# The first 45 microseconds of a two-layer trunk: load queues, zero products, and where layer 0's norm is summed

## The chip, the cores and the metric

The kernel runs on one core of a Trainium2 chip. The core has five engines that run side by side, each with its own ordered stream of instructions: TensorE (PE in the profile) for matrix products and transposes, VectorE (DVE), ScalarE (ACT) and GpSimd (POOL) for elementwise work, and SyncE (SP), which here only issues transfers. ACT and POOL can issue transfers too. An instruction waits for semaphores of the engines and transfers that it depends on, and whatever stands behind it on its engine waits with it.

The metric is the device time of one execution in microseconds, as the median of the runs. Before the change it is 995.59 us, over three runs of 995.08, 995.59 and 996.93 us.

## The reference, cut to what matters

The computation is a two-layer decoder trunk on 512 tokens of 1024 channels, in float32. Each layer has a mixer and a gated feed-forward network, each behind an RMS norm, and a last norm follows. The change touches layer 0's mixer only:

```python
xn = rms_norm(h, norm_mix[0])                 # h = x, the input
proj = jnp.einsum('bsd,de->bse', xn, w_in_even[0])        # 1024 -> 2048
a_b, a_c, a_v, z_b = proj[..., 0:512], proj[..., 512:1024], proj[..., 1024:1536], proj[..., 1536:]
y_a = a_b * causal_dwconv3(a_c * a_v, conv_a[0])
y_b = multiscale_pool(z_b, w_pool[0], pool_scale[0])      # windows 2, 4, 8, 16, one per group of 128 channels
h = h + jnp.einsum('bse,ed->bsd', jnp.concatenate([y_a, y_b], -1), w_out_even[0])
```

`multiscale_pool` takes for each group of 128 channels the mean over the last 2, 4, 8 or 16 tokens, less the token itself, and multiplies the result by a 128 x 128 matrix.

## The kernel before, in words

Activations are kept with channels on the 128 partitions and the 512 tokens along the row, so the 1024 channels are eight tiles, `k` = 0 to 7. Every float32 factor is split into a rounded high part and a low part (the residue), and a product of two tiles is three TensorE products: high by high, low by high and high by low (`mm3`, lines 146 to 149). ACT makes the high parts, DVE the low ones. A product accumulates in one of seven PSUM banks (`mm_bank`); an eighth, `aux_bank`, is for small things.

Work is written down in one order, and a scheduler orders each engine's instructions by priority and readiness within what the data allow. Instructions passed through `inorder` (or `order`) keep the order in which they were written on their engine. `behind` puts one instruction behind another on the same engine.

The kernel begins with eight products on zeros (the tile `idle`, lines 53 to 57), which nobody reads. Then layer 0's mixer (`mixer0`) starts:

- `load` fetches `x` in pieces (one tile, one tile, then pairs) and the matching rows of the weights of the z columns (1536 to 2047 of `w_in_even`). x goes over SP's queue. The first two weight pieces, z0 and z1, go over ACT's queue, the pairs over SP's. The norm's gain (`params_fetch`, 8 rows of 128) is fetched over ACT's queue behind z0.
- `turn(k)` transposes tile k of x on TensorE (four transposes of 128 x 128), turns the gain for k = 0, lets ACT write the high parts of the weights (`whi_z`) and of the scaled x (`hgh`) and DVE the low ones (`wlo_z`, `hgl`), copies x to `h`, and has ACT square a tile. POOL adds the squares up in `ssq`.
- `z_first` runs the products of k = 0 and 1 over the four column groups of z, with `turn(k + 1)` after the first four of each k. The general loop (`group`) does the rest, with `turn(k + 1)` ahead of each k. The last two k are done one column group after the other, so the four groups end one by one; each time `z_done(g)` is called.
- The normalization is not applied ahead of the products: the reciprocal root of the mean square is taken while they run. `rstd_cols` sums `ssq` over partitions by eight small products (the tile `ssc`, line 220) and takes the root on columns (ACT's square root, then DVE). `rstd_spread` turns the columns into a tile of all tokens by four transposes (`ssr`, line 210). Both use the `aux` bank. In `z_done`, `rstd_cols` is called at g = 1, `rstd_spread` and the pooling of groups 0 and 1 at g = 2, and the pooling of groups 2 and 3 behind their copies. `z_copy` takes a finished bank to SBUF on ACT; there are two such buffers. `z_pool` (DVE) scales it, builds the window sums by doubling, and splits the result into `pooled`.
- Then come the column groups `ac`, `av` and `ab` (512 columns each, with the same `group` loop over all eight k and the last four k done column by column). `c_done` evacuates `ac` on DVE (line 474), which needs the spread norm. Their weights come in four pieces of two k each into four `raw` buffers, which the splits free again.

Of the kernel before, what the change touches and what calls it, by code (L numbers as in the profile page):

```python
# [8 lines left out]
F32 = mybir.dt.float32  # L9
# [6 lines left out]
P = 128  # L16
D = 1024
S = 512
NK = D // P
# [3 lines left out]
EPS = 1e-6  # L23
WINDOWS = (2, 4, 8, 16)
PAD = 16
WARM = 8
LINE = 64
SHARE = 672

# [2 lines left out]
def tile_trunk(ctx: ExitStack, tc: tile.TileContext, x, norm_mix, norm_ffn, final_norm,  # L32
# [3 lines left out]
    nc = tc.nc  # L36
# [9 lines left out]
    def mm_bank(name):  # L46
        return ps_mm.tile([P, 512], F32, tag="mm", name=name)

    def aux_bank(name):
        return ps_aux.tile([P, 512], F32, tag="aux", name=name)  # L50


    idle = tp.tile([P, 512], BF16, tag="rstd", name="idle")
    nc.vector.memset(idle, 0.0)
    clock = aux_bank("clock")
    for i in range(WARM):
        nc.tensor.matmul(clock, idle[:, :P], idle, start=i == 0, stop=i == WARM - 1)

    ident = cp.tile([P, P], F32, name="ident")
    make_identity(nc, ident)  # L60
# [9 lines left out]
    def params1():  # L70
# [1 line left out]
            ("mix", rows_of(norm_mix[1]), NK), ("bsp", b_spatial[0], NK),  # L72
            ("ffn", rows_of(norm_ffn[1]), NK), ("cf", conv_rows(conv_ffn[1]), 3 * NF),
            ("bf", rows_of(b_conv_ffn[1]), NF)])

    inorder = tc.keep_in_program_order

    def behind(ins, first):

# [13 lines left out]
    def params_fetch(layer, rows_, queue):  # L93
        rows = sum(n for _, _, n in rows_)
        pk = cp.tile([P, P], F32, tag="pk", bufs=1, name=f"pk{layer}")
        at, views = 0, {}
        for key, ap, n in rows_:
            queue.dma_start(pk[at : at + n, :], ap)
            views[key] = at
            at += n  # L100

        def turned(order=lambda ins: ins):
            ps = aux_bank(f"prm_ps{layer}")
            order(nc.tensor.transpose(ps[:, :rows], pk[:rows, :], ident[:rows, :rows]))
            sb = cp.tile([P, P], F32, tag="prm0" if layer == "0" else "prm1", name=f"prm{layer}")
            nc.vector.tensor_copy(sb[:, :rows], ps[:, :rows])

            def col(key, i):
                return sb[:, views[key] + i : views[key] + i + 1]

            return col

        return turned

    def rows_of(ap):
        return ap.rearrange("(r p) -> r p", p=P)
# [2 lines left out]
        return ap.rearrange("w (r p) -> (w r) p", p=P)  # L119


    def fetch(src, a, b, name, queue=nc.sync):
        raw = wp.tile([P, a, b], F32, tag="raw", bufs=4, name=f"raw_{name}")
        queue.dma_start(raw, src)
        return raw, a, b, name

    def weights(src, a, b, name):
# [52 lines left out]
    def hg_k(k):  # L180
        return hg[k][0], hg[k][1]
# [124 lines left out]

    prm0 = prm1 = None

    def in_fetch(name, w, c0, k, n, queue=nc.sync):
        return fetch(w[k * P : (k + n) * P, c0 : c0 + 512].rearrange("(k p) c -> p k c", p=P),  # L310
                     n, 512, f"{name}_{k}", queue)

    def in_parts(chunks, k, raw, after=(None, None)):
        hi, lo = parts(*raw, after=after)
# [3 lines left out]
    def in_group(name, w, c0, lhs_is_weight, on_done, tail, chunks=None, before=None,  # L318
                 after=(None, None), begun=None):
        if chunks is None:  # L320
            chunks = {}
            for k in range(0, NK, 2):
                in_parts(chunks, k, in_fetch(name, w, c0, k, 2), after)

        def wt(k, j):
            cs = slice(j * P, (j + 1) * P)
            return chunks[k][0][:, cs], chunks[k][1][:, cs]

        def wt_wide(k, j):
            return chunks[k]  # L330

        def tokens(k, j):
            cs = slice(j * P, (j + 1) * P)
            return hg[k][0][:, cs], hg[k][1][:, cs]

        if lhs_is_weight:
            group(name, range(4), list(range(NK)), wt, lambda k, j: hg_k(k), tail, on_done, before,
                  begun=begun)
        else:
            group(name, range(4), list(range(NK)), tokens, wt_wide, tail, on_done, before)  # L340

    def mixer0():
        nonlocal prm0
        w = w_in_even[0]
        with tc.tile_pool(name="m0", bufs=1) as mp:
            prm_mix = {}
            norm = Norm("m0", lambda k: prm_mix["col"]("mix", k))
            zchunks = {}
            xt = {}
# [1 line left out]
            def load(k, n):  # L351
                t = mp.tile([P, NT, n * P], F32, tag="four", bufs=5, name=f"xt{k}")
                nc.sync.dma_start(
                    t, x[:, k * P : (k + n) * P].rearrange("(t p) d -> p t d", p=P))
                for i in range(n):
                    xt[k + i] = t[:, :, i * P : (i + 1) * P]
                raws[k] = in_fetch("z", w, 1536, k, n, nc.scalar if n == 1 else nc.sync)
                if k == 0:
                    prm_mix["turned"] = params_fetch(
                        "mix", [("mix", rows_of(norm_mix[0]), NK)], nc.scalar)  # L360

            raws = {}
            fed = [None, None]
# [7 lines left out]
            def turn(k):  # L371
                ps = mm_bank(f"xt_ps{k}")
                order = inorder if k < 2 else lambda ins: ins
                for t in range(NT):
                    order(nc.tensor.transpose(ps[:, t * P : (t + 1) * P], xt[k][:, t, :], ident))
                if k == 0:
                    prm_mix["col"] = prm_mix["turned"](inorder)
                if k in raws:
                    raw, a, b, name = raws.pop(k)
                    hi = wp.tile([P, a, b], F32R, tag="whi", bufs=6, name=f"whi_{name}")  # L380
                    lo = wp.tile([P, a, b], F32R, tag="wlo", bufs=6, name=f"wlo_{name}")
                    for i in range(a):
                        zchunks[k + i] = hi[:, i, :], lo[:, i, :], raw[:, i, :]
                whi, wlo, wraw = zchunks[k]
                inorder(nc.scalar.activation(whi, wraw, AF.Copy))
                g = prm_mix["col"]("mix", k)
                inorder(nc.scalar.activation(hg[k][0], ps, AF.Copy, scale=g))
                inorder(nc.vector.tensor_tensor(wlo, wraw, whi.bitcast(F32), ALU.subtract))
                fed[0] = inorder(nc.vector.scalar_tensor_tensor(
                    hg[k][1], ps, g, hg[k][0].bitcast(F32), op0=ALU.mult, op1=ALU.subtract))  # L390
                inorder(nc.vector.tensor_copy(h[k], ps))
                if k > 0:
                    norm.square(k - 1, put_square)
                if k == 0:
                    load(6, 2)
                elif k == NK - 1:
                    norm.square(k, put_square)
# [19 lines left out]
            W = S + PAD  # L417
            mix = {}
# [3 lines left out]
            zs = {}  # L422

            def z_copy(g, ps):
                zs[g] = mp.tile([P, S + LINE], F32, tag="z", bufs=2, name=f"z{g}")[:, :W]
                nc.gpsimd.memset(zs[g][:, :PAD], 0.0)
                nc.scalar.copy(zs[g][:, PAD:], ps)

            def z_done(g, ps):
                if g == 1:  # L430
                    norm.rstd_cols()
                elif g == 2:
                    rstd[0] = norm.rstd_spread()
                    z_pool(0)
                    z_pool(1)
                z_copy(g, ps)
                if g > 1:
                    z_pool(g)

            def z_pool(g):  # L440
                win, z = WINDOWS[g], zs[g]
                nc.vector.tensor_tensor(z[:, PAD:], z[:, PAD:], rstd[0], ALU.mult)
                s, step = z, 1
                while step < win:
                    s2 = mp.tile([P, S + LINE], F32, tag="zs", bufs=3, name=f"zs{g}_{step}")[:, :W]
                    lo_c = 2 * step - 1
                    nc.vector.tensor_tensor(s2[:, lo_c:], s[:, lo_c:], s[:, lo_c - step : W - step],
                                            ALU.add)
                    s, step = s2, 2 * step
                pl = mp.tile([P, S], F32, tag="pl", bufs=2, name=f"pl{g}")  # L450
                nc.vector.scalar_tensor_tensor(pl, s[:, PAD:], 1.0 / win, z[:, PAD:],
                                               op0=ALU.mult, op1=ALU.subtract)
                e = win - 1
                nc.vector.tensor_tensor(pl[:, :e], s[:, PAD : PAD + e], inv_pos[:, :e], ALU.mult)
                nc.vector.tensor_tensor(pl[:, :e], pl[:, :e], z[:, PAD : PAD + e], ALU.subtract)
                pooled[g] = split(mp, pl, f"pl{g}", tag="mix", bufs=8)
# [11 lines left out]
            ac = {}  # L468
# [6 lines left out]
                nc.gpsimd.tensor_tensor(t, t, rstd[0], ALU.mult)  # L475
                ac[j] = t

            in_group("ac", w, 512, True, c_done, 4, after=fed)

            cv = {}  # L480

# [12 lines left out]
            for g in range(4):  # L494
                ps = mm_bank(f"pm{g}")
# [644 lines left out]
    def down(name, ks, pieces, lhs, rhs, on_done):  # L1140

        for n, piece in enumerate(pieces):
# [4 lines left out]
            on_done(piece, ps)  # L1147

    n = mixer0()
    n = ffn0(n)  # L1150
    n = mixer1(n)
# [31 lines left out]
```

## Time and profile before

| what | value |
|---|---|
| median of three runs | 995.59 us |
| the profiled execution's own time | 996.99 us |
| span of the profiled execution, first to last instruction | 995.3 us |
| TensorE busy | 984.4 us (99%) |
| DVE, ACT, POOL busy | 728.5, 535.8, 104.1 us |
| first product on zeros starts | 1.26 us |
| first transpose of x starts | 6.08 us |
| first z product starts | 8.34 us |
| first z product of k = 2 starts | 17.79 us in the chain |
| norm sums (`ssc`) start | 34.94 us |
| first `ac` product | 37.95 us in the chain |

Times in the profile count from the first instruction of the program. A row of the timeline has the start, the duration, the engine, the line, the operation and its tiles; products are pipelined, so each one's duration overlaps the next one's start. The chain follows what ended last back to what released it, and gives each piece only the time that it added. A row of the waits has who waited for whom, the microseconds in total, how often, and the longest. Each row is of one execution, whose own time is 1.4 us above the median.

### The profile page before, as it was taken

Reading aid. Unit: us, or ns where it says so; the run is one execution under the profiler, and the core shown is the slowest. Engines: PE = TensorE matmul, PEld = TensorE weight load, DVE = VectorE, ACT = ScalarE, POOL = GpSimd, SP = SyncE. Lnnn points to the kernel's source line nnn. Section 1 sums busy time; section 2 is a strip of 40 time slices with the busy share of each in tenths; the row PEclk is TensorE's granted clock in tenths of the full one; section 3 lists DMA queues with packets and bytes.
Section 4 is the critical chain, followed back from the end, with each engine's and each line's share of the span. In section 5 each row is a group of like instructions: output and inputs, shape, how many; then the busy total and the mean of one; then the engine's idle time right before and its main releaser. Section 6 shows DMA issues by size and latency. Waiting matters only on the chain.

```text
span 995.3 us, 14922 instructions
## 1 busy us (share of the span) xinstructions
PE 984.4 (99%) x5899; PEld 877.1 (88%) x5899; DVE 728.5 (73%) x1104; ACT 535.8 (54%) x806; POOL 104.1 (10%) x121
## 2 busy tenths in 40 slices
PE   8999999999999999999999999999999999999997
PEld 6788888898999989999888988888989899898996
DVE  4797457968685886858988765399668868688686
ACT  4622346744663746637668734565546356463564
POOL 2222021200000000000211001202000010000100
PEclk9999999999999999999999999999999999999999
DMA  7342325454544644446432523345535456364542
GB/s 224 128 143 94 103 85 127 108 147 127 128 139 116 170 127 127 139 116 170 127 105 75 171 74 97 92 108 127 149 85 154 134 123 184 84 153 134 125 120 85
DMA packets 83073, 125.07 MB, mean 126 GB/s; under 512 B 4308, under 2 KB 56252, under 8 KB 83004
## 3 DMA queue, kind: packets, MB, share of 16 engines
q1 hardware_dynamic: 73740, 97.71, 31.0%
q0 software_dynamic: 7056, 23.60, 13.3%
q10 hardware_dynamic: 2208, 2.82, 0.9%
q8 instruction: 46, 0.75, 0.3%
q14 instruction: 23, 0.19, 0.1%
HBM read 98.42 MB, written 2.10 MB: 101 GB/s over the span
## 4 chain that ended last, share of the span: by engine, by line
PE 98%; DVE 1%; DMA 1%; ACT 0%; POOL 0%; issue 0%; DVEq 0%; ACTq 0%; POOLq 0%
PE d L147 4%; PE d L148 4%; PE d L149 4%; PE dn L147 4%; PE dn L148 4%; PE dn L149 4%; PE gu L147 3%; PE gu L148 3%; PE gu L149 3%; PE v L147 1%; PE oo L149 1%; PE oo L147 1%; PE v L149 1%; PE v L148 1%; PE oe L149 1%; PE oe L147 1%
## 5 line engine op out<-in xcount | busy, mean ns | idle before, releaser
L147 PE MATMUL dn<-whi_dn,a_hi 128*128 128x512 f32 (+1 forms) x180 | 69.4, 385 | 0.0
L148 PE MATMUL dn<-wlo_dn,a_hi 128*128 128x512 f32 (+1 forms) x180 | 69.3, 385 | 0.0
L148 PE MATMUL d<-a_lo,whi_d 128*128 128x512 f32 x176 | 68.6, 390 | 0.0
L149 PE MATMUL d<-a_hi,wlo_d 128*128 128x512 f32 x176 | 68.5, 389 | 0.0
L149 PE MATMUL dn<-whi_dn,a_lo 128*128 128x512 f32 (+1 forms) x180 | 67.9, 385 | 0.0
L147 PE MATMUL d<-a_hi,whi_d 128*128 128x512 f32 x176 | 66.9, 390 | 0.0
L561 DVE SCALAR_TENSOR_TENSOR c<-rows,prm,c 128x512 f32<-128x512 f32 x88 | 66.6, 768 | 0.0
L135 POOL DMA_DIRECT2D wlo_g<-raw_g x22 | 19.1, 866 | 373.9 <-ACT wlo_g L134 250.0
L1104 DVE TENSOR_TENSOR y<-dn,y 128x512 f32<-128x512 f32 (+1 forms) x49 | 32.6, 676 | 23.2 <-PE dn L149 22.7
L134 ACT ACTIVATE wlo_g<-raw_g 128x1024 fp32r<-128x1024 f32 x22 | 23.2, 1055 | 42.4 <-PE dn L148 42.4
L567 ACT ACTIVATE s<-c,prm 128x512 f32<-128x512 f32 x44 | 31.7, 720 | 20.6 <-DVE c L561 20.5
L674 DVE TENSOR_TENSOR wlo_s34u<-s34u,whi_s34u 128x1024 fp32r<-128x1024 f32 x18 | 22.1, 1225 | 27.8 <-ACT whi_s34u L673 27.8
L149 PEld LDWEIGHTS dn<-whi_dn,a_lo 128*128 128x128 f32 x180 | 33.8, 188 | 7.3 <-DVE a_lo L256 0.2
L673 ACT ACTIVATE whi_s12u<-s12u 128x1024 fp32r<-128x1024 f32 x18 | 18.9, 1050 | 39.3 <-PE d L148 33.7
L147 PEld LDWEIGHTS dn<-whi_dn,a_hi 128*128 128x128 f32 x180 | 33.8, 188 | 7.0 <-ACT a_hi L254 0.2
L148 PEld LDWEIGHTS dn<-wlo_dn,a_hi 128*128 128x128 f32 x180 | 33.8, 188 | 6.4
L148 PEld LDWEIGHTS d<-a_lo,whi_d 128*128 128x128 f32 x176 | 33.0, 188 | 7.2 <-DVE a_lo L256 0.2
L299 DVE TENSOR_TENSOR h<-d,h 128x512 f32<-128x512 f32 x48 | 32.6, 685 | 9.2 <-PE d L149 9.2
L147 PEld LDWEIGHTS d<-a_hi,whi_d 128*128 128x128 f32 x176 | 32.8, 188 | 7.0
L149 PEld LDWEIGHTS d<-a_hi,wlo_d 128*128 128x128 f32 x176 | 33.0, 188 | 6.8
L254 ACT ACTIVATE a_hi<-s 128x512 fp32r<-128x512 f32 x44 | 27.6, 628 | 16.2 <-DVE s L746 7.4
L143 DVE TENSOR_TENSOR wlo_dn<-raw_dn,whi_dn 128x1024 fp32r<-128x1024 f32 x22 | 26.8, 1221 | 11.6 <-ACT whi_dn L142 11.6
(1273 smaller groups left out, 3472.4 us busy)
## 6 DMA issues: line engine op xcount, KB each, us to landing
raw_g<-in_w_ffn_gate_dram SPq DMA_DIRECT2D x36, 512.0 KB
raw_u<-in_w_ffn_up_dram SPq DMA_DIRECT2D x36, 512.0 KB
wlo_g<-raw_g POOLq DMA_DIRECT2D x22, 512.0 KB, 4.7
raw_d<-in_w_ffn_down_dram SPq DMA_DIRECT2D x22, 512.0 KB
raw_dn<-in_w_ffn_down_dram SPq DMA_DIRECT2D x22, 512.0 KB
wlo_u<-raw_u POOLq DMA_DIRECT2D x19, 512.0 KB, 4.6
raw_oe<-in_w_out_even_dram SPq DMA_DIRECT2D x8, 512.0 KB
raw_g<-in_w_ffn_gate_dram SPq DMA_DIRECT2D x16, 256.0 KB
```

Source lines behind the costliest of these rows:

```text
L134: first = nc.scalar.activation(lo, raw, AF.Copy, scale=-1.0)
L135: nc.gpsimd.dma_start(lo, raw, accum_op=ALU.add)
L143: behind(nc.vector.tensor_tensor(lo, raw, hi.bitcast(F32), ALU.subtract), after[0])
L147: nc.tensor.matmul(ps, lhs[0], rhs[0], start=start, stop=False)
L148: nc.tensor.matmul(ps, lhs[0], rhs[1], start=False, stop=False)
L149: nc.tensor.matmul(ps, lhs[1], rhs[0], start=False, stop=stop)
L254: nc.scalar.activation(hi, src, AF.Copy, scale=scale)
L299: nc.vector.tensor_tensor(h[k], ps, h[k], ALU.add)
L561: nc.vector.scalar_tensor_tensor(c, t[:, i : S + i], prm("cf", i * NF + ft), c, op0=ALU.mult, op1=ALU.add)
L567: nc.scalar.activation(s, c, AF.Silu, bias=self.prm("bf", ft))
L674: nc.vector.tensor_tensor(lo, src, hi.bitcast(F32), ALU.subtract)
L1104: nc.vector.tensor_tensor(dst, ps, dst, ALU.add)
```

## The change

Three things change, all at the start of layer 0's mixer or ahead of it.

The loads: z0 and z1 go over SP's queue, between the pieces of x, and the gain's load over ACT's queue becomes the first thing that `mixer0` issues. SP's first loads are then x0, z0, x1, z1, x2/x3, z2/z3, x4/x5.

The products on zeros: there are nine instead of eight, now kept in program order ahead of the first transposes, and five more of 256 columns stand between the transpose of the gain and the first z product.

The norm: `rstd_cols` is called at g = 2 instead of g = 1, and `rstd_spread` and all four poolings ahead of k = 1 of `ac`. The copies of z get four buffers instead of two, the window sums two instead of three. The mixer's results are the same.

```diff
-WARM = 8
+WARM = (9, 512)
+STAY = (5, 256)
...
-    clock = aux_bank("clock")
-    for i in range(WARM):
-        nc.tensor.matmul(clock, idle[:, :P], idle, start=i == 0, stop=i == WARM - 1)
+    def keep_busy(bank, n, cols):
+
+        for i in range(n):
+            inorder(nc.tensor.matmul(bank[:, :cols], idle[:, :P], idle[:, :cols], start=i == 0,
+                                     stop=i == n - 1))
+
+    keep_busy(aux_bank("clock"), *WARM)
...
-            prm_mix = {}
+            prm_mix = {"turned": params_fetch("mix", [("mix", rows_of(norm_mix[0]), NK)],
+                                              nc.scalar)}
...
-                raws[k] = in_fetch("z", w, 1536, k, n, nc.scalar if n == 1 else nc.sync)
-                if k == 0:
-                    prm_mix["turned"] = params_fetch(
-                        "mix", [("mix", rows_of(norm_mix[0]), NK)], nc.scalar)
+                raws[k] = in_fetch("z", w, 1536, k, n)
...
                 if k == 0:
                     prm_mix["col"] = prm_mix["turned"](inorder)
+                    keep_busy(mm_bank("busy"), *STAY)
...
-                zs[g] = mp.tile([P, S + LINE], F32, tag="z", bufs=2, name=f"z{g}")[:, :W]
+                zs[g] = mp.tile([P, S + LINE], F32, tag="z", bufs=4, name=f"z{g}")[:, :W]
...
             def z_done(g, ps):
-                if g == 1:
+                if g == 2:
                     norm.rstd_cols()
-                elif g == 2:
+                z_copy(g, ps)
+
+            def pool_all(k):
+                if k == 1:
                     rstd[0] = norm.rstd_spread()
-                    z_pool(0)
-                    z_pool(1)
-                z_copy(g, ps)
-                if g > 1:
-                    z_pool(g)
+                    for g in range(4):
+                        z_pool(g)
...
-                    s2 = mp.tile([P, S + LINE], F32, tag="zs", bufs=3, name=f"zs{g}_{step}")[:, :W]
+                    s2 = mp.tile([P, S + LINE], F32, tag="zs", bufs=2, name=f"zs{g}_{step}")[:, :W]
...
-            in_group("ac", w, 512, True, c_done, 4, after=fed)
+            in_group("ac", w, 512, True, c_done, 4, after=fed, before=pool_all)
```

## The prediction

> **What bounds the kernel now.** I read the page's busy times and chain first, then the list of what TensorE waited for, then the chain and TensorE's own timeline over the first 60 us.
>
> ```profile
> span 995.3 us, 14922 instructions
> ...
> PE 984.4 (99%) x5899; PEld 877.1 (88%) x5899; DVE 728.5 (73%) x1104; ACT 535.8 (54%) x806; POOL 104.1 (10%) x121
> ...
> PE 98%; DVE 1%; DMA 1%; ACT 0%; POOL 0%; issue 0%; DVEq 0%; ACTq 0%; POOLq 0%
> ```
>
> TensorE (PE) is the bound, and the chain lies on it for 98% of the span. Its waits, all of them:
>
> ```profile
> PE clock L57 <- DVE idle L54: 1.3, 1, 1.3
> PE xt_ps L375 <- DMA xt<-in_x_dram: 1.2, 1, 1.2
> PE z L410 <- ACT hgh L387: 1.0, 1, 1.0
> PE ssc_m L220 <- POOL ssq_m L203: 0.5, 1, 0.5
> ```
>
> There are four waits in 995 us, all in layer 0's mixer, and the change touches three of them. After 36 us PE never waits. A microsecond won before that reaches the end unless the change makes a new wait. The chain over that stretch (start, duration):
>
> ```profile
> 0.81 5.13 DMA xt<-in_x_dram
> 5.94 0.14 issue
> 6.08 1.08 PE xt_ps L375 x4
> ...
> 8.34 2.07 PE z L410 x4
> 10.42 0.85 PE xt_ps L375 x4
> 11.27 3.79 PE z L410 x12
> 15.06 0.44 PE xt_ps L375 x4
> 15.50 1.86 PE z L410 x8
> 17.36 0.44 PE xt_ps L375 x4
> 17.79 0.23 PE z L147
> ...
> 33.60 1.30 POOL ssq_m L203
> 34.90 0.04 issue
> 34.94 1.05 PE ssc_m L220 x8
> ```
>
> The reader is to see the same work at two prices: four transposes take 0.85 us and later 0.44, a product 0.23 us from 17.79 on and far more before. The timeline shows where the price changes:
>
> ```profile
> 10.92 2.06 PE L410 MATMUL z<-hgh,wlo_z 128*128 128x512 f32 x4
> 12.78 1.38 PE L410 MATMUL z<-hgl,whi_z 128*128 128x512 f32 x4
> 13.99 1.07 PE L410 MATMUL z<-hgh,whi_z 128*128 128x512 f32 x4
> 14.90 0.60 PE L375 MATMUL xt_ps<-ident,xt 128*128 128x128 f32 x4
> ```
>
> Start to start, the first four take 1.86 us (0.43 each after the first), the next 1.21, the third 0.91 (0.23 each). With prices of 0.43 and 0.23, 1.21 us is one and a half products at the old price, so PE doubled its pace at about 13.4. That is 5.1 us after 8.34, where PE's work became unbroken. The granted clock is 1.00 throughout these windows; it does not show this step.
>
> **The change, part by part.** The sum is against the profiled execution: span 995.3, its own time 996.99, which is 1.4 us above the median of 995.59.
>
> *Loads.* The weight tiles z0 and z1 move from ACT's queue into SP's, and the gain row is now ACT's only early load. The first transposes wait for x0 alone. In the first 4.75 us both queues moved 0.58 MB, ACT's 0.27 of it beside x0. Cumulating that window's rates, the 0.26 MB of x0, now ahead of everything, is through by about 3.6; it landed 1.2 us after the last bytes of the first pair then, so I estimate 4.0 to 4.8 instead of 5.94. But the zero products now stand in PE's order ahead of the transposes: nine at 0.43 us from 1.26 (eight took 3.59 with the last one's tail) let the next instruction start at 5.1. So the transposes start at about 5.2, not 6.08: -0.9, ends 0 (x0 no earlier) and -1.0.
>
> What is moved later: SP issues cost about 0.5 us each (three in 1.53), so the issues of x2/x3, z2/z3 and x4/x5 slip by 1.0 us, to 2.9, 3.4 and 3.9. By then the queues still hold over 1 MB. Cumulated bytes in the new order (0.58 MB by 4.75, 0.29 more by 6, 0.75 more by 8, then 0.37 a us) put z0 at 4.6, x1 at 5.7, z1 at 6.5, x2/x3 at 7.9 and z2/z3 at 9.3. With 1.2 us to land, z0 is there by 5.8, and its split (0.63 on ACT) ends by 6.5, before ACT can scale x0 (6.7 below). The others have 1.4 us or more. Cost nothing.
>
> *Zeros.* Five 256-column zero products follow the gain's transpose. PE stood still between that transpose (7.09) and the first real product (8.34) for VectorE's copy (0.17) and ACT's scaling (0.69). Half of 0.43 is 0.21 each, 1.07 in all, which fits into those 1.25 us; cost nothing, up to 0.2 if ACT is early. What they and the ninth product do is to leave PE no gap from 1.26 on. If 5.1 us of unbroken work double the pace here too, that falls at 6.4, during the zeros, with x0's transposes done at the old price. The first product then starts 2.2 us after the transposes (2.27 before; 1.75 if even these are quick: 0.4 less transposing, 0.1 less for the gain): 7.4. -0.1, ends 0 and -0.5.
>
> From the first product to k=2's first, 8.34 to 17.79, is 9.45 us: 24 products and three sets of transposes. At the quick prices, 24 x 0.23 + 3 x 0.44 = 6.85. -2.6, ends 0 (pace as late as now) and -2.6. What could be late next is VectorE: per k it does a split of 0.69, a residue of 0.75 and a copy of 0.68, and PE now needs k=1's residue 5.5 us after its first product; by these rows it is done 2.9 after. ACT's hgh of k=1 follows its transposes by 0.7 and is needed 1.8 after them. Both hold.
>
> The Trainium skill, "TensorE: Matmul & The Clock Gate", Part 1, says that the half-rate clock is released after a busy window of about 3.4 us that runs freely; from 1.26 on that would give an estimate of 4.7 to 8.1, the earlier end worth 0.5 more than my sum and the later 0.35 less. The measured 5.1 us lies between one and two such windows, so the trace agrees.
>
> *Norm sums.* The eight ssc products waited 0.52 us for POOL. In the built order they move behind the third bank's last two products: 2 x 0.23 = 0.46 of the wait is filled. -0.46, ends -0.52 and 0. The work after is tighter. ssc's end to the first ac product was 1.95 us; now six z products and the parameter transpose (0.1) stand between, 1.6. ACT's split of ac's first weights is queued behind the square root: it ended 1.4 after ssc's end (36.34 + 1.05), just in time. VectorE's residue of these weights now stands behind the parameter copy, which waits for that transpose: copy at 1.8, residue (1.23) done at 3.15 to 3.2. PE wants it after six products, at 3.05. +0.15, ends 0 and +0.3.
>
> *Pooling.* The spread of the norm moves behind k=0 of ac, and all pooling with it. All four residues of ac come first on VectorE, so pooling starts 5.1 us after ac's first product (3.0 before), with 1.2 us of residue already done. VectorE was full from 36 to 70 us, so it runs about 1 us late. Who waits: ac's evacuations free the bank that av's fourth column needs. The first took place at 55.56; av starts at 60.4 and needs the bank nine products later, 62.4. The built order puts it six instructions earlier. Slack 6 us: cost nothing. z2 and z3 are copied out at once (four buffers instead of two), which frees two banks that were held till 46.8 and 49.0; nobody waited for them. POOL's two extra border clears fall before its sums; SP's raw_av loads slip behind three small parameter issues (about 1.2 us), 15 us before av needs them. Nothing.
>
> Sum: -0.9 - 0.1 - 2.6 - 0.46 + 0.15 = -3.9. Off the profiled 996.99 that is 993.1, off the median 991.7. The runs of before spread over 1.85 us, as much as 3.7 us of half-pace work cost, so part of the profiled run's excess may be a late doubling which the change removes; the rest would stay in a profile. Between the two I take **992.2**, 0.34% less.
>
> **Rivals.** About 0.2% (2.0 us) is what a measurement can tell from no change: the line is 993.6.
>
> *The pace doubles late.* Zeros, transposes or a small gap before x0 may not count. If it is counted from the first real product, 7.4 + 5.1 = 12.5: 2.55 of the 2.6 come back in cold products, and -0.9 - 0.1 - 0.05 - 0.3 = -1.35 is left: 994.2. If a gap at x0 restarts it at 6.08, the products start at 8.3, double at 11.2: -1.5, 994.1. For it: eight zeros over 3.6 us did not double the pace in before. Against: they were too short by the 5.1 us measured, and the stretch that did work had transposes in it (10.21). The skill's same page, Part 4, says that transposes do not count as busy for the clock; the row at 10.21 speaks against that. By that as a mechanism here, counting from the five zeros at 6.2 gives 11.3, -1.9, 993.7. All three together: 0.2.
>
> *One queue is too slow, and the result is slower.* In 4.75 to 6.0 SP's queue moved 0.21 MB in 1.25 us, 0.168 MB a us, while ACT's ran beside it. If that is its own limit with rows this short, the 2.1 MB to z2/z3 pass at 14.4 and land at 15.5; with the splits k=2 starts near 17, PE stands 2.5 us idle from 14.3, and if the pace falls back another 5.1 us at half pace cost 2.55: 997.0, and 999.5 if x4/x5 do it again. I take 998. It decides where z2/z3 land after about 13. Against: between 14.7 and 15.9 SP's queue alone moved 0.36 MB, mostly such short rows, at 302 GB/s. 0.07.
>
> *VectorE becomes the bound.* Were pooling so late that the first evacuation slips past 62.4, each us beyond the 6 of slack costs one; 8 us late gives 994.2. The built order speaks against it: 0.05.
>
> **How the numbers follow.** Forecast 0.68, the others 0.2, 0.07 and 0.05. The forecast's own range is 991.0 (all the best ends: -4.6 off the median) to 993.3. The range over the cases, 991.0 to 994.3, leaves out the slow queue and the edges. Faster: nearly all of the first case and a third of the late doubling, 0.74; slower 0.07; same 0.19.
>
> **What would show it.** In the changed profile: transposes at 5.0 to 5.4; the first z product at about 7.4 with 0.23 us a product; k=2 starting at 14.2 to 14.6; no wait for POOL at ssc, or under 0.1; a wait of up to 0.3 at the first wlo_ac product; no other PE wait. Wrong would be products of 0.43 after 9 us, a wait for raw_z or xt beyond the first, or a wait for av's bank.

## The result, and the profile after

| | median us | lowest to highest | runs |
|---|---|---|---|
| before | 995.53 | 993.52 to 997.05 | 22 |
| after | 994.28 | 993.81 to 994.83 | 22 |

The ratio is 0.9985, with an interval of 0.9978 to 0.9991: about 1.5 us less (1.25 between the medians). The kernel is faster, but by less than the 0.2% line. The forecast was 3.4 us less. The profiled execution of after took 994.15 us, its span is 992.4. One fact is needed to read all times of before: they lie in three groups 1.4 to 1.6 us apart (near 993.7, 995.3 and 996.7), while those of after are one group. The execution that was profiled before, 996.99, is of the highest.

The page of after, busy times, the chain's shares, and TensorE's waits, which answer to the lines shown of before:

```profile
span 992.4 us, 14934 instructions
...
PE 982.9 (99%) x5905; PEld 875.6 (88%) x5905; DVE 728.5 (73%) x1104; ACT 536.3 (54%) x806; POOL 105.3 (11%) x121
...
PE 94%; issue 1%; DVE 1%; DMA 1%; ACT 0%; DVEq 0%; POOLq 0%; ACTq 0%
```

```profile
PE clock L62 <- DVE idle L57: 1.3, 1, 1.3
PE u_20b L535 <- DMA wlo_u<-raw_u: 0.8, 1, 0.8
PE z L415 <- ACT hgh L392: 0.4, 1, 0.4
```

The columns of the waits are total, count and longest, in us. The waits for x0 (1.2) and for POOL at `ssc` (0.5) are gone, and that for the first `hgh` fell from 1.0 to 0.4. But there is a new one of 0.8, for a weight tile of the second network, far from every line of the diff. TensorE's timeline of after (start, duration, then what ran; in brackets the idle time before):

```profile
1.26 3.99 PE L62 MATMUL clock<-idle 128*128 128x512 bf16 x9 [1.26 <-DVE idle L57]
5.07 0.62 PE L379 MATMUL xt_ps<-ident,xt 128*128 128x128 f32 x4
5.62 0.22 PE L110 MATMUL prm_psmix<-ident,pkmix 8*128 8x8 f32 x1
5.78 0.72 PE L62 MATMUL busy<-idle 128*128 128x256 bf16 x5
6.94 1.20 PE L415 MATMUL z<-hgh,whi_z 128*128 128x512 f32 x4 [0.45 <-ACT hgh L392]
...
13.82 0.48 PE L153 MATMUL z<-hgh,whi_z 128*128 128x512 f32 x1
```

Transposes at 5.07, the first four quick already (0.62 us against 1.08), the first product at 6.94, and k = 2 at 13.82, against 17.55 in the same row of before. Comparing the same instruction in both traces, TensorE is 3.73 us ahead at k = 2 and 3.8 ahead from 45 to 954 us. There, in the last unit of layer 1's network, the lead falls to 2.86 and stays. The chain of after at that place, start and duration:

```profile
942.24 6.62 issue
948.86 0.02 POOLq L1184
948.88 5.94 DMA wlo_u<-raw_u
954.81 0.04 issue
954.86 1.46 PE u_20b L535 x10
```

So two questions were open. Why did a transfer at 949 us become late? And why is the gain against the runs half of what the profiles show?

### The profile page after: what moved, and what is told of

The parts are those of the page before. It is cut to its first block, busy times and chain, and to the rows that moved or that the text cites. A ratio compares the mean times of both kernels' runs of the same rounds, so it can differ in the third digit from the quotient of the medians.

```text
span 992.4 us, 14934 instructions
## 1 busy us (share of the span) xinstructions
PE 982.9 (99%) x5905; PEld 875.6 (88%) x5905; DVE 728.5 (73%) x1104; ACT 536.3 (54%) x806; POOL 105.3 (11%) x121
## 4 chain that ended last, share of the span: by engine, by line
PE 94%; issue 1%; DVE 1%; DMA 1%; ACT 0%; DVEq 0%; POOLq 0%; ACTq 0%
PE d L154 4%; PE d L153 4%; PE d L155 4%; PE dn L153 4%; PE dn L154 4%; PE dn L155 4%; PE gu L153 3%; PE gu L154 3%; PE gu L155 3%; PE v L153 1%; PE oo L155 1%; PE oo L153 1%; PE v L155 1%; PE oe L155 1%; PE oe L154 1%; PE v L154 1%
```

## Experiments: the wait at 954 us

`wlo_u` is made by a transfer which POOL issues and which adds `raw_u` onto a tile that ACT filled. It landed in 4.97 us before and in 5.94 after. During it, the DMA engines differ in one thing, which the DMA view of the two traces shows, each from the issue to the last data packets. Before, to 957.1 us:

```profile
q0 software_dynamic: 143, 0.52, 63.1%
...
wlo_u<-raw_u POOLq DMA_DIRECT2D x1, 512.0 KB, 5.0
```

After, to 954.8 us:

```profile
q0 software_dynamic: 144, 0.52, 47.5%
q8 instruction: 1, 0.02, 1.0%
...
wlo_u<-raw_u POOLq DMA_DIRECT2D x1, 512.0 KB, 5.9
```

q0 carries the transfer; q8 carried one packet of 16 KB in after's window. The page counts 46 packets on q8 with 0.75 MB in all, and TensorE has 11,810 instructions (products and weight loads), 257 a packet: q8 brings TensorE its code. The Trainium skill, "Runtime: NRT & Kernel Launch", section "Instruction fetch mechanics", says the same of the size (blocks of 16 KiB, 256 instructions) and that crossing a block is mostly hidden. The size agrees. For TensorE's own stream the cost is hidden here, too, but not for a transfer that meets the fetch. The transfer ends with 16 small packets, as many as there are DMA engines; in after's trace 15 of them came by 4.2 us after the issue and the last at 5.65, while in between single data packets passed one behind the other. The window from 953.1 to 954.7 us of after has five packets, which fill 5.7% of 16 engines, that is 0.9 of one:

```profile
q0 software_dynamic: 5, 0.02, 5.7%
```

So about one engine's share was left when the others were done, and it ended 1.5 us behind them. The change adds 12 TensorE instructions (one zero product and five more, each with its load), which moves each fetch against the work. The packet started 4.49 us after the issue before, when the data was nearly through, and 3.02 us after it in after.

The theory to test: it is the count of instructions that makes this wait, not the loads, the norm sums or the earlier time. Its rival: whatever makes TensorE earlier makes this transfer late.

**The transfer taken away.** In layer 1's f = 20 the low part of `u` is made by VectorE's subtraction (`parts`) instead of the adding transfer, first in after:

```diff
-                hi, lo = summed(*raws[key, 1])
+                hi, lo = (parts if (key, layer, f) == ("u", 1, 20) else summed)(*raws[key, 1])
```

Beside it a second execution of after, unchanged, was profiled, and the same edit was made in before.

> The changed kernel once more, on the chip of the next three. Theory A (the late wait): TensorE again waits 0.8 to 0.9 us for wlo_u of the last unit near 954 us and the time is again about 994.3. Theory B (luck of the clock in before): the wait at 954 was an accident of one execution, here below 0.3 us, and the time is still about 994.3, because what is missing lies in the kernel before, whose clock doubles at 13.4 us in some executions and one stretch earlier in others. Both: the doubling of TensorE's pace at 5 to 7 us, the first product of k=2 at 13.8 to 14.6.

> The changed kernel, but the up-weights of the last unit of the second feed-forward network are split by ACT and VectorE instead of ACT and an accumulating transfer of GpSimd, so that TensorE cannot wait for that transfer. Theory A: the 0.8 to 0.9 us come back, 993.4. Theory B: no change, 994.3 (within 0.3).

> The kernel before with the same replacement. Theory A: before has no such wait in its profile, so no change, 995.5 with its two groups of times at 995.2 and 996.6. If before has the wait in those executions that are quick at the start, the lower group falls by up to 0.9 us, to 994.3, and the upper one stays.

Measured, with the runs of before of the same set at 995.88: after again 994.50 (0.9983, 0.9974 to 0.9992), its wait for `wlo_u` 0.9 us; after with the edit 993.92 (0.9977, 0.9967 to 0.9986); before with the edit 995.88 (0.9999, 0.9990 to 1.0008). The waits of after with the edit:

```profile
PE clock L62 <- DVE idle L57: 1.3, 1, 1.3
PE u_20e L535 <- DVE wlo_s12u L679: 0.3, 1, 0.3
```

The wait is gone, and 0.6 us of the median with it, less than theory A's 0.9. The extra work on VectorE makes a smaller wait, 0.3 for itself, and takes 0.4 of lead; in before it costs these 0.4 and wins nothing in the trace. Together that is about 1 us for the late transfer in after, and nothing in before.

**The count alone, in before.** Before's eight zero products of 512 columns become two of 512 and twelve of 256: the same time on TensorE, and 12 instructions more, as many as the change adds.

```diff
-WARM = 8
+WARM = (512, 512) + 12 * (256,)
-    for i in range(WARM):
-        nc.tensor.matmul(clock, idle[:, :P], idle, start=i == 0, stop=i == WARM - 1)
+    for n in WARM:
+        nc.tensor.matmul(clock[:, :n], idle[:, :P], idle[:, :n], start=True, stop=True)
```

> Before, but its eight zero products of 512 columns are fourteen (two of 512, twelve of 256 columns): the same time on TensorE, 12 more TensorE instructions, as many as the change adds. Theory C (a block of TensorE's code is fetched every 256 instructions, and the shifted fetch falls into the last unit's accumulating transfer and delays it): a fetch starts 1.5 to 4 us after that transfer's issue, TensorE waits 0.7 to 1.0 us for wlo_u near 957 us, the median rises by 0.8, to 996.5. Rival (the wait comes from the earlier start itself): no wait at 957, median as before.

Its waits, all but the first three, which are those of before:

```profile
PE ssc_m L220 <- POOL ssq_m L203: 0.5, 1, 0.5
PE u_20b L530 <- DMA wlo_u<-raw_u: 0.5, 1, 0.5
```

Twelve instructions, without any of the change, bring the wait into before: the fetch starts 1.64 us after the issue and the transfer lands in 5.60. The wait is smaller than the 0.7 to 1.0 expected. The rival falls: TensorE comes to this place only 0.14 us earlier than in before (the product ahead starts at 957.46 here, at 957.60 there), not 3.8 as in after. In before the transfer landed at 957.66 and the product that needs it started at 957.72: no wait shows there, but the slack was 0.06 us. The median, 996.84 against 995.54, says little, since both kernels' times lie in three groups; the ratio is 1.0006 (0.9995 to 1.0016). Within the lowest group the runs are at 994.5 to 994.75 against 993.45 to 993.87, about 0.95 us more.

**The count in after, moved on.** The same zeros in pieces of 128 columns, 64 instructions more and the same time on TensorE:

```diff
-WARM = (9, 512)
-STAY = (5, 256)
+WARM = (36, 128)
+STAY = (10, 128)
```

> After, with the zeros cut smaller: 36 products of 128 columns for nine of 512, ten of 128 for five of 256, the same time on TensorE and 64 more instructions. Theory C: the fetch near the end of the last unit starts some 3 to 4 us earlier than in after, is over before the accumulating transfer moves, the wait for wlo_u is below 0.2 us, and the time falls by 0.6 to 0.9, to 993.5. Rival: the wait of 0.8 to 0.9 stays and so does the time, 994.4.

Measured 993.36 us (992.74 to 993.45), ratio 0.9976 (0.9967 to 0.9985). All waits, and the DMA view from the issue of `wlo_u` (949.2 us) to 954:

```profile
PE clock L62 <- DVE idle L57: 1.3, 1, 1.3
PE z L415 <- ACT hgh L392: 0.3, 1, 0.3
```

```profile
q0 software_dynamic: 144, 0.52, 57.7%
issues: line engine op xcount, KB each, median us to landing
wlo_u<-raw_u POOLq DMA_DIRECT2D x1, 512.0 KB, 4.5
```

No code packet (it came 0.9 us ahead of the issue), 4.5 us to land, no wait. Its slowest run is 0.36 us under the fastest of after's 22, which are of another set. In all twelve traces that have this transfer (the last five kernels come in the next section) the landing goes by where the packet falls:

| kernel | TensorE instructions over before | code packet starts after issue, us | landing, us | wait, us |
|---|---|---|---|---|
| before; again; again | 0 | 4.49; 4.56; 4.54 | 4.97; 4.93; 4.91 | none |
| after; again | 12 | 3.02; 1.65 | 5.94; 6.06 | 0.8; 0.9 |
| before, 12 more | 12 | 1.64 | 5.60 | 0.5 |
| after, 64 more | 76 | none within | 4.53 | none |
| loads alone; norm sums alone | 0 | 4.67; 4.44 | 5.04; 4.95 | none |
| zeros alone | 12 | 1.59 | 5.94 | 0.8 |
| after, 64 more, without the loads; without the norm part | 76 | none within | 4.52; 4.53 | none |

## Experiments: where the gain at the start comes from

Each part of the change was put into before alone: the zeros (nine, and five behind the gain), the loads, and the norm sums with the pooling.

> Before with the zeros alone (nine in order, five more behind the gain); loads and norm as before. If the zeros bring the doubling: transposes at 6.0 to 6.1 as before, pace doubled by 8 us, k=2 at 14.3 to 14.9 instead of 17.8, ssc still waiting 0.5 us for POOL. Time 994.0 to 994.9 with theory A's late wait, 993.3 to 994.0 without it, and in one group, not two. If the doubling needs the earlier x0 as well: 995.0 or more, in two groups.

> Before with the loads alone on SP's queue; zeros and norm as before. x0 is no longer shared with: transposes at 4.9 to 5.3 instead of 5.6 to 6.1, first z product at 7.1 to 7.6. Pace doubled 5.1 us after the first unbroken product or one 3.4 us window earlier. Time 0.4 to 1.0 below before, still in two groups 1.5 us apart; if z0 behind x0 comes late, nothing is won.

> Before with the later norm sums and pooling alone. The ssc wait for POOL falls from 0.5 to below 0.1, a wait of 0 to 0.3 for the residue of ac's first weights appears, no wait for a bank of av. Time 0.2 to 0.4 below before, in its two groups. If pooling so late made VectorE the bound, PE would wait after 60 us and the time would rise.

The core of the three edits:

```diff
 zeros
-WARM = 8
+WARM = (9, 512)
+STAY = (5, 256)
...
+                    keep_busy(mm_bank("busy"), *STAY)
 loads
-                raws[k] = in_fetch("z", w, 1536, k, n, nc.scalar if n == 1 else nc.sync)
+                raws[k] = in_fetch("z", w, 1536, k, n)
 norm sums and pooling
-                if g == 1:
+                if g == 2:
                     norm.rstd_cols()
...
-            in_group("ac", w, 512, True, c_done, 4, after=fed)
+            in_group("ac", w, 512, True, c_done, 4, after=fed, before=pool_all)
```

| part alone | median us | ratio (interval) | TensorE's lead at 45 us in its trace | 
|---|---|---|---|
| zeros | 994.95 | 0.9991 (0.9983 to 1.0000) | 3.2 |
| loads | 994.02 | 0.9987 (0.9978 to 0.9996) | 2.1 |
| norm sums, pooling | 996.38 | 1.0001 (0.9991 to 1.0011) | 0.6 |

The lead is against the profiled execution of before; of the 0.6 of the last row, 0.5 is there at k = 2 already, where this part has done nothing: x0 landed 0.3 us earlier and the pace doubled earlier in that execution. The zeros alone have 12 instructions more and so the wait at `wlo_u`, 0.8 us; without it they would be at about 994.0, as the loads are. The loads alone won 1.3 to 1.5 us, more than the 0.4 to 1.0 expected. Their twelve runs lie in two groups, seven at 993.2 to 994.2 and five at 995.0 to 995.8, and the trace (995.17 us) is of the slower five, so its lead of 2.1 holds for these alone. What the loads do is seen in their trace:

```profile
1.26 3.60 PE L57 MATMUL clock<-idle 128*128 128x512 bf16 x8 [1.26 <-DVE idle L54]
4.65 1.06 PE L373 MATMUL xt_ps<-ident,xt 128*128 128x128 f32 x4
5.64 0.27 PE L104 MATMUL prm_psmix<-ident,pkmix 8*128 8x8 f32 x1
7.25 2.08 PE L408 MATMUL z<-hgh,whi_z 128*128 128x512 f32 x4 [1.34 <-ACT hgh L385]
```

x0 is there by 4.65 instead of 5.94. But the first product starts at 7.25 only, after 1.34 us of idle: `hgh` stands on ACT behind the split of z0 (5.99 us, 5.13 in before), which now arrives behind x0 on the same queue. Of 1.43 us that the transposes won, the products got 1.09.

The norm sums lose their wait for POOL, and TensorE's lead grows by 0.08 us from 33 to 45 us, not by the 0.31 forecast. In after it grows by 0.07 over the same stretch.

To see the parts without the wait at 954, each of the two others was undone in the version with 64 more instructions.

> The version with 64 more small zeros and the late norm sums, but the loads as before (z0 and z1 on ACT's queue, the gain behind z0). Theory: the early x0 is worth little, since z0 then gates the first product, but it closes the gap after the zeros. So transposes at 5.5 to 6.1, first z product at 7.4 to 7.7, most executions within 0.3 of the version with the loads (993.4), and some, where the gap delays the doubling, 1.4 to 1.8 above. Rival (the loads are worth the 0.9 us that was forecast): all executions 0.7 or more above, 994.1.

> The same version with the loads and the zeros, but the norm sums and the pooling as before. By the traces so far (from 33 to 45 us the norm part gains 0.07 us), the time is 993.4 to 993.5, as with it. By the forecast's -0.3 it is 993.7. The wait for POOL at ssc is 0.5 and there is none for wlo_ac.

Measured, beside runs of before at 995.37: without the loads 993.49 (0.9983, 0.9974 to 0.9992), without the norm part 993.60 (0.9980, 0.9971 to 0.9989), against 993.36 with both. By these medians, given the zeros, each of the other two is worth 0.1 to 0.2 us, but the 993.36 is of a set on another chip, and the runs do not resolve so little. The traces give more for the loads: against before's profiled execution TensorE's lead at 45 us is 3.45 with both, 3.09 without the loads and 3.37 without the norm part. Without the loads TensorE waits for x0 as in before (0.8 us against 1.2), and the first product starts at 7.66, 0.35 later than with them:

```profile
PE xt_ps L381 <- DMA xt<-in_x_dram: 0.8, 1, 0.8
PE z L417 <- ACT hgh L394: 0.3, 1, 0.3
```

None of its eleven runs (993.13 to 994.04) lies 1.4 us above the rest, as some were expected to.

## Experiments: the three groups of before

If the zeros are worth 2.6 us, why is the gain against the runs 1.5? The theory: the groups are executions in which TensorE doubles its pace at different times. Two more executions of before, unchanged, were profiled to catch other groups:

> The kernel before once more, to catch an execution of its quicker groups in a profile. Theory B: an execution near 995.2 shows the doubling of the pace some 3.4 us earlier than 13.4, near 10, one near 993.6 two such steps earlier, near 6.6; one near 996.7 shows 13.4 again. Rival: the groups differ elsewhere and the doubling is at 13.4 in each.

> The kernel before a further time, for the same purpose and with the same expectation: the doubling near 13.4, 10 or 6.6, and the time near 996.7, 995.2 or 993.6 with it.

They came out at 995.53 and 994.00 us, one from each of the lower two groups. TensorE's timeline of the first:

```profile
5.96 0.63 PE L375 MATMUL xt_ps<-ident,xt 128*128 128x128 f32 x4 [1.24 <-DMA xt<-in_x_dram]
6.51 0.22 PE L104 MATMUL prm_psmix<-ident,pkmix 8*128 8x8 f32 x1
7.71 1.97 PE L410 MATMUL z<-hgh,whi_z 128*128 128x512 f32 x4 [0.98 <-ACT hgh L387]
9.48 1.05 PE L375 MATMUL xt_ps<-ident,xt 128*128 128x128 f32 x4
10.19 1.67 PE L410 MATMUL z<-hgh,wlo_z 128*128 128x512 f32 x4
11.69 1.09 PE L410 MATMUL z<-hgl,whi_z 128*128 128x512 f32 x4
```

And of the second:

```profile
5.98 0.63 PE L375 MATMUL xt_ps<-ident,xt 128*128 128x128 f32 x4 [1.13 <-DMA xt<-in_x_dram]
6.54 0.22 PE L104 MATMUL prm_psmix<-ident,pkmix 8*128 8x8 f32 x1
7.74 1.19 PE L410 MATMUL z<-hgh,whi_z 128*128 128x512 f32 x4 [0.98 <-ACT hgh L387]
8.77 0.60 PE L375 MATMUL xt_ps<-ident,xt 128*128 128x128 f32 x4
```

Same program, same waits. In the second the pace has doubled before x0's transposes (0.63 us for four) and stays so. In the first it has doubled by then too, falls back at about 7.9, after two idle stretches of 1.24 and 0.98 us, and doubles again at about 11.3. In the execution shown with the prediction it doubled once, at 13.4. Against that one TensorE's lead is 2.9 us at k = 2 in the second and 1.4 in the first, and it keeps these to the end (2.99 and 1.47). So the theory holds for these three traces, one of each group; the expected moments of doubling did not: 11.3 was not foreseen as a second one, and the second trace had doubled before 6.0, not near 6.6.

That the pace is TensorE's clock is seen in the first of the two. The granted clock is the third figure from the end of a row of windows:

```profile
6.00:8.00 2.00, 1.02 (x6) 0.76 (x7) 1.08 (x3) 1.03 (x2) 0.00 (x0) 0.97 1.08 383
8.00:10.00 2.00, 2.00 (x7) 1.51 (x7) 1.64 (x3) 0.18 (x1) 0.00 (x0) 0.50 1.07 374
10.00:12.00 2.00, 2.00 (x9) 1.68 (x8) 0.70 (x2) 1.43 (x3) 0.00 (x0) 0.68 1.07 369
```

What is missing from 1.00 makes 3.4 us at a clock of 0.50. Ahead of the first doubling the rows show 1.00 whatever the pace, so there the pace is read from the products. The fall-back also marks the group in runs without a trace, since 3.4 us at half the clock take 0.002 off an execution's mean. The mean clock is on record for 86 runs of before: it is 0.997 in all 37 of the middle group, 0.999 in all 38 of the highest, and 0.998 (ten) or 0.999 (one) in the lowest.

The Trainium skill, "TensorE: Matmul & The Clock Gate", Part 1, says that the activity window of about 3.4 us runs freely, so the same kernel shows different counts of slow products from run to run. The rows agree: the stretch at half the clock lasted 3.4 us, as long as that window, and groups 1.4 to 1.6 us apart are half-pace stretches that differ by 2.8 to 3.2 us.

Over all 108 runs of before that accompany these kernels, 12 lie in the lowest group, 48 in the middle and 48 in the highest. Of the 63 runs, in five sets, of kernels that have both the zeros and the new loads, none lies apart from its set; of the 22 with the zeros alone or with the old loads, 3 do (996.4 to 996.6 in the zeros alone). In those two TensorE still stands idle for x0 before the transposes, 0.3 and 0.8 us in their traces. With before's eight zeros and the new loads alone the trace has no such gap, and seven of the twelve runs are some 1.7 us under the other five; a doubling ahead of the first product would win them 1.4 (half of the 2.8 us from 7.25 to 10.1). In before only 12 of 108 are in the lowest group. That the gap is what delays the doubling fits both, but it was not tried by itself, and no trace of those seven runs was kept.

## Why the prediction was right or wrong

**The loads.** Transposes forecast at about 5.2, measured 5.07. The step "cost nothing" for z0 held in three of the five traces with the zeros and the new loads and failed in two. It was put at 5.8, with its split done by 6.5, before x0 could be scaled. The split starts when z0 is there: at 5.6 to 5.8 in three traces, and ACT's scaling then starts at 6.57, behind the gain's copy and not behind z0. In after's trace z0 came as forecast, at 5.69, but the transposes were quick and the gain's copy was done at 6.05; ACT's scaling started at 6.22, 0.2 us late. In the second execution of after z0 came at 6.47 and the scaling at 7.01, 0.6 us late. TensorE's waits of 0.4 and 0.9 us for `hgh` have these delays in them. Given the zeros, the loads are worth 0.35 us in the traces and 0.1 by the medians, not the 0.9 forecast.

**The zeros.** Right in the sum, and for the reason given, against the execution it was reckoned from: 0.9 + 0.1 + 2.6 forecast up to k = 2, 3.73 measured. The terms were not all right. The transposes won 1.01, the way from there to the first product 0.39 (in this execution the pace doubled before the transposes), and the way on to k = 2 won 2.33. The 2.6 was too large, since its 9.45 us ends at the chain's row of that product (17.79); from timeline row to timeline row 9.21 became 6.88. In the other four traces with the zeros and the new loads the pace doubled later, and the lead at k = 2 was 2.9 to 3.4. The premise of "5.1 us of unbroken work" was not a constant. In the seven traces with the zeros the pace doubles between about 4.7 and 7.3 us (5.07 at the latest in after's), 3.4 to 6.0 us after the first zero product; with the loads alone at about 10.1, 2.8 us after the first product. The forecast 6.4 lies among these, and all seven come before the products that matter, so the error cost little.

**The norm sums.** The sum -0.46 + 0.15 was mis-sized: 0.07 measured. The wait shrank by 0.45, as forecast. VectorE's residue of ac's first weights was late, as forecast, but cost 0.28 (0.16 idle before 35.36 and 0.12 in the three products that follow), near the upper end of 0.3. Another 0.1 went with the parameter transpose, which costs that much more at its new place, between z and `ac`, than among the products of `ac`. TensorE's and VectorE's rows of after:

```profile
34.97 0.40 PE L154 MATMUL ac<-hgl,whi_ac 128*128 128x512 f32 x1
35.36 0.97 PE L155 MATMUL ac<-hgh,wlo_ac 128*128 128x512 f32 x3
36.17 0.39 PE L153 MATMUL ac<-hgh,whi_ac 128*128 128x512 f32 x1
```

```profile
33.90 0.27 DVE L112 COPY prm<-prm_ps 128x112 f32<-128x112 f32 x1
34.09 4.79 DVE L149 TENSOR_TENSOR wlo_ac<-raw_ac,whi_ac 128x1024 fp32r<-128x1024 f32 x4
```

**The pooling.** Right: it starts at 38.8, and nobody waits.

**The end of the path.** "A microsecond won before that reaches the end unless the change makes a new wait" was the step that named the danger, and the search for new waits stopped at layer 0's mixer. The new wait came at 954 us, by the count of instructions, which the prediction did not price at all: 0.95 us. A list of waits does not show how near a wait is; here the slack was 0.06 us.

**From the profile to the median.** "Between the two I take 992.2" failed most. The sum of -3.9 off the profiled 996.99 gives 993.1; with the wait of 0.95 it would be 994.0, and 994.15 was measured. Off the median it does not hold, since in 12 of the 22 executions the pace had doubled earlier without help. Against the middle group the change wins about 1.0 us, against the highest 2.4, and against the lowest it loses 0.7. The prediction saw that part of the profiled run's excess might be a late doubling, but subtracted a part of the full gain from the median all the same.

**The rivals.** In no trace with the zeros did the pace double as late as 11 to 12.5. One queue was not too slow: no z product after the first waits for weights. VectorE did not become the bound. The time, 994.28, came out 0.02 under the upper end of the range, and that is luck: this end was set by the late doubling and by VectorE as the bound, neither of which came, while the causes, a gain taken off the wrong executions and a code packet, stood in none of the rivals.

**The better version** is the change with its zeros in pieces of 128 columns: 993.36 us, 2.2 under before's median of that set (0.3 under its lowest group), with the same work at the start and no code packet in the late transfer.

## What to carry to other kernels

When the times of a kernel fall in groups, find out which group the profiled execution belongs to before a sum is taken off it: a change that makes a lucky event certain is worth its full price against the unlucky runs only. A change in the number of TensorE's instructions moves its code packets along the whole program, and where a transfer has little slack, such a packet can use it up; a few instructions more or less, at no time of their own, tell this from a real cost. When the first of two loads is brought forward on a shared queue, price the second as the new gate.

## What the runs showed of the hardware that was not expected

- A 16 KB code packet for TensorE delays a 512 KB adding transfer that it meets: landing at 5.6 to 6.1 us against 4.5 without one and 4.9 to 5.0 with one at its tail. By the closing packets all but one of the DMA engines finish as usual. The packets that met it in mid-transfer took 1.0 to 1.5 us, and the landing came 1.1 to 1.5 us later than without one. It happens elsewhere without harm: in after, the transfer issued at 356.9 us met a packet 2.42 us after its issue and landed in 5.76, against 4.75 in before, where the packet came at 4.42, and TensorE did not wait for it. SP's loads ran beside both.
- Eight zero products and a gap of 1.1 to 1.2 us were enough to have the pace doubled before the transposes in two of three traces of before, and not in the third, nor in the three traces of other versions with zeros for the same time and a gap of 0.7 to 1.1 us (before with 12 more instructions, before with the edit at f = 20, the norm sums alone).
- The granted clock can fall back to 0.50 for 3.4 us after two short gaps of about 1 us each within 3 us, with the first real products just begun. In another execution of the same kernel the same two gaps left it at 1.00.
